# A decoder layer's output projection: operand sums and weight lo parts on VectorE, embedding lo parts by adding DMAs, weight sums in smaller steps

## The chip, the cores and the metric

One core of one Trainium2 chip. The metric is the device time of one execution in microseconds; a figure for a kernel is the median of several runs. The engines are named as in the profile: PE (TensorE matmul), PEld (its weight loads), DVE (VectorE), ACT (ScalarE), POOL (GpSimd) and SP (SyncE, which here only issues DMAs). "SPq", "ACTq" and "POOLq" are DMA issues of these engines. Every engine runs its own row of instructions in order.

## What is computed

One layer of a decoder trunk over 1024 positions of width 1024, all in float32: three kinds of attention heads side by side, whose 1024 outputs go through `w_out`; then a gated MLP with a causal convolution; then a gate on a per-layer embedding.

```
z = rmsnorm(h, norm_mix_g[l]) @ w_in[l]
...
o_a = hgrn2_mix(a_q, a_f, a_i, a_g, lbs[l], hgrn_gnorm_g[l])
o_b = dilated_window_mix(b_q, b_k, b_v)
...
h = h + jnp.concatenate([o_a, o_b.astype(o_a.dtype), o_c.astype(o_a.dtype)], axis=-1) @ w_out[l]
h = h + conv_glu_ffn(rmsnorm(h, norm_ffn_g[l]), ffn_up[l], ffn_conv_w[l], ffn_conv_b[l], ffn_down[l])
gate = jax.nn.sigmoid(rmsnorm(h, norm_ple_g[l]) @ ple_gate[l])
h = h + gate * (p[l] @ ple_proj[l])
```

## The kernel before

Activations lie transposed, 128 channels by 1024 positions to a tile (`T`), in halves of 512 (`HT`). Every float32 operand of a matmul is split in a hi part, which ACT casts (L124 for weights, L1296 for activations, L1482 for the embedding), and a lo part, the rest of it. A product is then three matmuls: hi x hi, lo x hi, hi x lo. For weights, `split2` makes the lo part in one of two ways. Given an engine, that engine subtracts (L130). Given a DRAM address, ACT negates the hi part (L127), and a POOL DMA adds the weight from DRAM once more onto it (L128).

The kernel's stages, with their times in the profile: the RWKV heads with the `w_in` projection (`project_rest`, to about 330 us), the other heads (to 572), the output projection (`phase_out`, to 661), part of the embedding product (`embed`, to 682), the MLP (up to about 1300), the gate.

**Output projection.** `w_out` is applied by seven products of half size instead of eight (Strassen's way), on sums of the operands and of the weight blocks. There are 28 jobs, in the order p1, p5, p3, p6, p7, p2, p4 with four blocks each, and every job is 12 matmuls of 128x512, 2.72 us on PE without waits. Job n's weight is loaded and split when job n - 4 is run (`weight`, L1342). The raw weights lie in halves of a ring of two 512 KB tiles (`wraw`); the four raw tiles of the embedding (`praw`) use the same ring, between the weights of jobs 18 to 27. Jobs of the products p1, p6, p7 and p4 run in banks that lie in pairs in one PSUM tile, so that the second job of a pair starts only behind the `gather` of the first, a DVE addition to the residual `h` (L1387). Gathers of p6 and p7 are followed by a square on ACT (L232) and its addition to `acc` on DVE (L233); PE sums `acc` over the channels (L200), DVE and POOL make the factor of the norm (L203, L207) and PE spreads it (L213). This is done once for the first half of the positions behind job 20, and once for the second half inside `embed`.

The work beside a job stands in a table: `at(n, steps)` puts step i behind job n + i. `pair` casts and subtracts to make hi and lo parts of an operand. `o_done`, called where a head group's output is ready, makes sums of operands for the first four blocks (`Eo[i]`, by a DVE subtraction and two ACT negations) and, for the last four, two POOL DMAs that add one block to the negated one (L1320, SBUF to SBUF). `turn4` subtracts on DVE for p4. `ffn_first` (L1534) loads the first four 512 KB tiles of `ffn_up` and splits them; it is put behind a job of the projection.

**Weight sums.** `out_sums` is a generator that builds four sums of `w_out` blocks for each of four block rows, in DRAM-loaded tiles: loads on SP (L457, L458), ACT negations in place, POOL DMAs that add (L455), and stores to the DRAM buffers `ws..` on SP (L463, L466, L475, L476). `project_rest` takes one step of it after k-steps 1, 3 and 6 of the eight of a `w_in` block. Beside it, on the same SP row, stand the loads of `w_in` (L115), the moves of the projections `z` (L505), and the two moves Tz (L743) and Tc (L748) by which a triangular matrix of the RWKV heads passes through DRAM. PE's L848 waits for Tc.

## Time and profile before

| | |
|---|---|
| median of 3 runs | 1424.47 us (1424.16 to 1427.31) |
| the profiled execution | 1429.45 us |
| its span in the trace | 1427.7 us |
| mean granted clock of TensorE | 0.985 |
| PE busy | 1376.9 us (96%) |
| DVE busy | 1062.1 us (74%) |
| ACT busy | 663.1 us (46%) |
| POOL busy | 382.5 us (27%) |
| bytes moved by DMA | 195.93 MB |

PE is busy for 96% of the span, so what is left to win are its waits and the time at which the throttle grants it less than full clock. A matmul group's row in the timeline gives start, length, what it writes and reads, how often it stands there (x2), and in square brackets how long PE was idle ahead of it and whose end released it. A row of the waits sums such idle time by the waiting line and the releaser. The row of a window gives busy time of each engine in a stretch, then the granted clock (1.00 is full) and the share of time in which the 16 DMA engines were busy.

### The profile page before, as it was taken

To read this page: it belongs to the slowest core of one execution; us is meant where nothing else is said; L and a number is where in the kernel's file an instruction comes from. 1 tells how busy PE (TensorE), PEld (TensorE's weight loads), DVE (VectorE), ACT (ScalarE), POOL (GpSimd) and SP (SyncE) were. 2 spreads that over 40 slices of the span, in tenths; PEclk is the share of its full clock that TensorE was granted. 3 is DMA by queue.
4 is the path that set the end of the run, shared out by engine and by line. 5 is a ranking of instruction groups with operands and counts; after the bars stand their busy time and mean duration, and the time that the engine had idled before them with its cause. 6 is when DMAs were issued, how large, how long until landed. Compare 5 with 4: busy or idle time off the path is not lost.

```text
span 1427.7 us, 22537 instructions
## 1 busy us (share of the span) xinstructions
PE 1376.9 (96%) x8598; PEld 1114.9 (78%) x8598; DVE 1062.1 (74%) x1652; ACT 663.1 (46%) x1143; POOL 382.5 (27%) x312
## 2 busy tenths in 40 slices
PE   8999999989999999988999999999999999999997
PEld 6878777867878777766788888888888888888886
DVE  7595456815657696667988889888988799777675
ACT  7523424233255584554644444344444444455662
POOL 4210112211221222321244445454543000002231
PEclk9999999999999999997999999999999999999998
DMA  6344533774732223894323232333233973352674
GB/s 227 89 118 112 134 111 92 176 168 115 237 116 97 90 65 84 212 295 124 137 74 107 101 109 97 111 111 110 89 111 119 353 243 104 109 164 62 174 194 146
DMA packets 98843, 195.93 MB, mean 137 GB/s; under 512 B 22064, under 2 KB 24368, under 8 KB 98736
## 3 DMA queue, kind: packets, MB, share of 16 engines
q1 hardware_dynamic: 73408, 155.44, 32.1%
q0 software_dynamic: 14256, 27.79, 11.0%
q10 hardware_dynamic: 11072, 11.28, 2.5%
q8 instruction: 67, 1.10, 0.3%
q14 instruction: 40, 0.33, 0.1%
HBM read 141.78 MB, written 50.59 MB: 135 GB/s over the span
## 4 chain that ended last, share of the span: by engine, by line
PE 51%; POOL 0%; DVE 0%; issue 0%; DMA 0%; POOLq 0%; ACT 0%; DVEq 0%
PE bg L1501 16%; PE bv L1501 12%; PE bv L1803 7%; PE bg L1803 7%; PE bv L152 1%; PE bv L154 1%; PE bv L156 1%; PE bg L152 1%; PE bg L156 1%; PE bg L154 1%; DMA raw<-in_ffn_up_dram 0%; PE dp L154 0%; PE dp L152 0%; PE dp L156 0%; POOL h L1892 0%
## 5 line engine op out<-in xcount | busy, mean ns | idle before, releaser
L130 POOL TENSOR_TENSOR wlo<-raw,whi 128x512 fp32r<-128x512 f32 x84 | 136.2, 1640 | 75.5 <-ACT whi L124 75.5
L124 ACT CAST whi<-wraw 128x512 fp32r<-128x512 f32 x120 | 73.3, 617 | 156.8 <-PE dp L154 99.8
L152 PE MATMUL dp<-xh,whi 128*128 128x512 f32 x416 | 139.6, 411 | 2.8 <-ACT xh L424 2.0
L154 PE MATMUL dp<-xl,whi 128*128 128x512 f32 x416 | 132.9, 394 | 0.9 <-DVE xl L425 0.9
L1501 PE MATMUL bg<-t,whi 128*128 128x512 f32 x352 | 133.2, 389 | 0.0
L156 PE MATMUL dp<-xh,wlo 128*128 128x512 f32 x416 | 132.4, 393 | 0.0
L130 POOL TENSOR_TENSOR wlo<-s,whi 128x512 fp32r<-128x512 f32 x44 | 65.4, 1486 | 170.0 <-ACT whi L124 170.0
L124 ACT CAST whi<-raw 128x512 fp32r<-128x512 f32 x88 | 52.6, 619 | 97.4 <-issue 51.5
L1803 PE MATMUL bg<-t,whi 128*128 128x512 f32 x308 | 95.1, 390 | 0.0
L1803 PE MATMUL bv<-t,whi 128*128 128x512 f32 x308 | 94.9, 389 | 0.0
L124 ACT CAST whi<-s 128x512 fp32r<-128x512 f32 x66 | 38.9, 619 | 118.8 <-PE bg L1501 113.5
L154 PEld LDWEIGHTS dp<-xl,whi 128*128 128x128 f32 x416 | 78.8, 189 | 18.8 <-DVE xl L425 1.8
L156 PEld LDWEIGHTS dp<-xh,wlo 128*128 128x128 f32 x416 | 78.4, 189 | 18.9 <-issue 1.5
L152 PEld LDWEIGHTS dp<-xh,whi 128*128 128x128 f32 x416 | 75.2, 190 | 22.9 <-issue 5.6
L1501 PEld LDWEIGHTS bg<-t,whi 128*128 128x128 f32 x352 | 66.0, 188 | 13.7
L207 POOL TENSOR_TENSOR rst<-rst,mhalf 128x4 f32<-128x4 f32 (+1 forms) x9 | 10.2, 1134 | 239.6 <-DVE rst L203 223.8
L128 POOL DMA_DIRECT2D wlo<-in_w_in_dram x28 | 25.3, 915 | 179.4 <-ACT wlo L127 156.4
L1799 ACT CAST t<-t 128x512 fp32r<-128x512 f32 x77 | 47.8, 622 | 45.7 <-PE bv L1803 32.6
L1501 PE MATMUL bg<-t,wlo 128*128 128x512 f32 x176 | 67.3, 389 | 0.0
L1803 PEld LDWEIGHTS bv<-t,whi 128*128 128x128 f32 x308 | 57.8, 188 | 12.0
L1803 PEld LDWEIGHTS bg<-t,whi 128*128 128x128 f32 x308 | 57.8, 188 | 11.9
L1800 DVE TENSOR_TENSOR t<-t,t 128x512 fp32r<-128x512 f32 x77 | 54.9, 713 | 8.0 <-ACT t L1799 7.8
(463 smaller groups left out, 3731.7 us busy)
## 6 DMA issues: line engine op xcount, KB each, us to landing
raw<-in_ffn_up_dram SPq DMA_DIRECT2D x44, 512.0 KB, 3.4
wraw<-in_w_in_dram SPq DMA_DIRECT2D x28, 512.0 KB, 3.8
z<-zst SPq DMA_DIRECT2D x18, 512.0 KB, 3.4
gb<-ct SPq DMA_DIRECT2D x33, 256.0 KB, 2.3
t<-gb SPq DMA_DIRECT2D x33, 256.0 KB, 2.8
t<-gt SPq DMA_DIRECT2D x33, 256.0 KB, 2.7
zl<-z SPq DMA_DIRECT2D x16, 512.0 KB, 4.4
wraw<-in_ple_gate_dram SPq DMA_DIRECT2D x16, 512.0 KB, 3.7
```

Source lines behind the costliest of these rows:

```text
L124: self.cast = nc.scalar.copy(hi, src).ins
L128: nc.gpsimd.dma_start(lo, eng, accum_op=ALU.add)
L130: eng.tensor_tensor(lo, src, hi.bitcast(F32), ALU.subtract)
L152: nc.tensor.matmul(ps[hf], wh, xh[hf], start=first, stop=False)
L154: nc.tensor.matmul(ps[hf], wh, xl[hf], start=False, stop=False)
L156: self.step = nc.tensor.matmul(ps[hf], wl, xh[hf], start=False, stop=last).ins
L207: nc.gpsimd.tensor_tensor(r2, r, self.mhalf[:, :n], ALU.pow)
L1501: self.step = nc.tensor.matmul(ps, w[part == 2][:, s], X[k][part == 1], start=start and k == part == 0, stop=k == 3 and part == 2, skip_gr ...
L1799: nc.scalar.copy(xh, x)
L1800: V.tensor_tensor(xl, x, xh.bitcast(F32), ALU.subtract)
L1803: nc.tensor.matmul(ps[m], wt[part == 2][:, m * P:(m + 1) * P], (xh, xl)[part == 1], start=k == part == 0, stop=k == NK - 1 and part == 2)
```

## The change

Five edits. The weight sums (`out_sums`) start after 9 pauses and not 15, are taken after every odd k-step (four to a block and not three), and one block row takes 14 steps and not 7, with pauses between loads, negations, adds and stores. In `o_done` one of the two ACT negations goes, the other becomes a copy, and the two POOL DMAs go; in their place `less` subtracts on DVE in `phase_out`, ahead of the pairs that use the sum. These pairs start behind jobs 6, 13 and 10 in place of 7, 10 and 11, and `turn4` behind job 16 in place of 12. All 28 weights of the projection get their lo part from DVE; so far the last twelve got it by L127 and L128. The embedding's lo parts are now negated on ACT and completed by an adding POOL DMA from DRAM (new L1489 and L1490), and no longer subtracted on DVE. `ffn_first` moves from behind job 15 to behind job 23.

```diff
--- before.py
+++ after.py
@@ -115,7 +115,7 @@
         nc.sync.dma_start(raw, src)
         return self.split_w(raw, src)
 
-    WB = 6
+    WB, LEAD = 6, 9
 
     def split2(self, src, eng):
 
@@ -442,37 +442,43 @@
 
         nc, wo = self.nc, self.a["w_out"]
         self.S = [{n: self.zpool.tile([P, HT], F32, tag=f"ws{n}{i}", name=f"ws{n}{i}") for n in "1234"} for i in range(4)]
-        for _ in range(15):
-            yield
+        def pause(n):
+            for _ in range(n):
+                yield
+
+        def turn(x):
+            nc.scalar.activation(x, x, AF.Copy, scale=-1.0)
+
+        def add(x, src):
+            nc.gpsimd.dma_start(x, src, accum_op=ALU.add)
+
+        yield from pause(self.LEAD)
         for i in range(4):
             a11, a12, a21, a22 = (wo[m][:, c] for m in (i, 4 + i) for c in (slice(0, HT), slice(HT, T)))
             t, u = (self.spool.tile([P, HT], F32, tag="sqt", name=self.nm("wsum"), bufs=2) for _ in (0, 1))
-
-            def turn(x):
-                nc.scalar.activation(x, x, AF.Copy, scale=-1.0)
-
-            def add(x, src):
-                nc.gpsimd.dma_start(x, src, accum_op=ALU.add)
-
             nc.sync.dma_start(t, a21)
             nc.sync.dma_start(u, a22)
-            yield
+            yield from pause(2)
             turn(t)
             add(u, a21)
             yield
+            add(t, a11)
+            yield from pause(2)
             nc.sync.dma_start(self.S[i]["1"], u)
-            add(t, a11)
             yield
             nc.sync.dma_start(self.S[i]["3"], t)
+            yield
             turn(u)
             yield
             turn(t)
             add(u, a11)
             yield
             add(t, a22)
+            yield
             add(u, a12)
+            yield from pause(2)
+            nc.sync.dma_start(self.S[i]["2"], t)
             yield
-            nc.sync.dma_start(self.S[i]["2"], t)
             nc.sync.dma_start(self.S[i]["4"], u)
             yield
 
@@ -489,7 +495,7 @@
                 self.mm3({0: ps[:, :HT], 1: ps[:, HT:]}, w(k), self.X[k], k == 0, k == ND - 1)
                 if k == 3 and i + 1 < len(js):
                     nxt = self.load_w(self.a["w_in"][js[i + 1]])
-                if k in (1, 3, 6):
+                if k % 2:
                     with self.behind(self.step):
                         next(self.sums, None)
                 yield
@@ -1309,15 +1315,12 @@
             nc.vector.tensor_tensor(t1, o[1], o[0], ALU.subtract)
             self.pair(self.A[i], o[0])
             self.pair(self.B[i], t1)
-            nc.scalar.activation(t1, t1, AF.Copy, scale=-1.0)
-            nc.scalar.activation(t3, o[1], AF.Copy, scale=-1.0)
+            nc.scalar.copy(t3, o[1])
             return
         i = self.LAST.index(k)
         for c in (0, 1):
             if (k, c) not in self.parts:
                 nc.scalar.copy(self.final(k, c, None), o[c])
-        for t in self.Eo[i][::-1]:
-            nc.gpsimd.dma_start(t, self.parts[k, 1], accum_op=ALU.add)
 
     def phase_out(self, hp, x0, emb):
 
@@ -1340,7 +1343,7 @@
                 hold.extend((t[:, left], t[:, right]))
             t, d = hold.pop(0), src[n](i)
             nc.sync.dma_start(t, d)
-            return self.split2(t, V if (n, i) in jobs[:16] else d)
+            return self.split2(t, V)
 
         g1 = [self.dps.tile([P, T], F32, tag="dp", name=self.nm("dp")) for _ in (0, 1)]
         banks = {"a": {i: g1[i // 2][:, (left, right)[i % 2]] for i in range(4)}, "b": {}, "c": {}}
@@ -1390,6 +1393,9 @@
                 if n in ("p6", "p7"):
                     sums(m, late)
 
+        def less(i, n):
+            V.tensor_tensor(Eo[i][n], Lo[i][1], Eo[i][n], ALU.subtract)
+
         def turn4(i):
             V.tensor_tensor(Lo[i][0], Lo[i][0], Eo[i][0], ALU.subtract)
 
@@ -1403,10 +1409,10 @@
         at(5, [lambda i=i: (empty("p1", i), load("p3", i)) for i in range(4)])
         at(16, [lambda i=i: load("p4", i) for i in range(4)])
         at(3, [lambda i=i: self.pair(D[i], Lo[i][1]) for i in range(4)])
-        at(7, [lambda i=i: self.pair(A[i], Eo[i][0]) for i in range(4)])
-        at(10, [lambda i=i: self.pair(C[i], Lo[i][0]) for i in range(4)])
-        at(11, [lambda i=i: self.pair(B[i], Eo[i][1]) for i in range(4)])
-        at(12, [lambda i=i: turn4(i) for i in range(4)])
+        at(6, [lambda i=i: (less(i, 0), self.pair(A[i], Eo[i][0])) for i in range(4)])
+        at(13, [lambda i=i: self.pair(C[i], Lo[i][0]) for i in range(4)])
+        at(10, [lambda i=i: (less(i, 1), self.pair(B[i], Eo[i][1])) for i in range(4)])
+        at(16, [lambda i=i: turn4(i) for i in range(4)])
         at(17, [lambda i=i: self.pair(A[i], Lo[i][0]) for i in range(4)])
         px, pw = [], []
         r = []
@@ -1446,7 +1452,7 @@
         for m in range(ND):
             sums(m, 1)
         ps, pb = small()
-        with self.behind(self.ends[15]):
+        with self.behind(self.ends[23]):
             self.ffn_first()
         r = []
         hooks = {(1, 0): lambda: r.append(self.rstd(ps, (acc,))), (1, 1): lambda: self.rstd_spread(r[0], pb)}
@@ -1480,7 +1486,8 @@
         hi, lo = (pool.tile([P, T], F32R, name=self.nm(n)) for n in ("peh", "pel"))
         for c in (slice(0, HT), slice(HT, T)):
             self.nc.scalar.copy(hi[:, c], raw[:, c])
-            self.nc.vector.tensor_tensor(lo[:, c], raw[:, c], hi[:, c].bitcast(F32), ALU.subtract)
+            self.nc.scalar.activation(lo[:, c], hi[:, c].bitcast(F32), AF.Copy, scale=-1.0)
+            self.nc.gpsimd.dma_start(lo[:, c], self.a[src][k][:, c], accum_op=ALU.add)
         dst.append((hi, lo))
 
 
```

Three places of the engines' rows show what moves; the lines of the changed program lie a few further on (L1296 becomes L1302, L1387 L1390, L1389 L1392, L1482 L1488, L1520 L1527, L1527 L1534).

The first is ACT's row around job 20, the last of p2. `peh` and `pel` are hi and lo parts of the embedding, here of `ple_proj`; `sqt` with `h7` is the last square of the first half, `whi` and `wlo` belong to the weight of job 23, `hd` are copies of `h` to DRAM. Before:

```order
L124 CAST whi_1118_6485<-wraw_1111_6449 128x512
L1389 DMA hd7_0_5953<-h7_5938 128x512
L127 ACTIVATE wlo_1119_6487<-whi_1118_6485 128x512
L232 ACTIVATE sqt_1120_6504<-h7_5938 128x512
L1296 CAST xh_897_5386<-xh_921_5410 128x512
L1389 DMA hd0_1_5940<-h0_5931 128x512
L1482 CAST peh_1116_6478<-praw_1115_6476 128x512 x2
```

After:

```order
L124 CAST whi_1118_6477<-wraw_1111_6439 128x512
L1302 CAST xh_897_5386<-xh_921_5410 128x512
L1488 CAST peh_1116_6468<-praw_1115_6466 128x512 x2
L1489 ACTIVATE pel_1117_6469<-peh_1116_6468 128x512 x2
L1392 DMA hd7_0_5941<-h7_5926 128x512
L232 ACTIVATE sqt_1120_6495<-h7_5926 128x512
```

The last square of the first half stood ahead of the cast of the embedding, and stands behind it and its negation now; the negation of the weight is gone.

The second is DVE's row from the gather of job 23 (L1387, from the tile `zo`) to that of job 24 (from `dp`); the rows between are parts of the norm of the first half (L1527) and the lo parts `t` of its results (L1520). Before:

```order
L1387 TENSOR_TENSOR h3_5934<-h3_5934,zo_1144_6619 128x512
L1527 SCALAR_TENSOR_TENSOR h2_5933<-h2_5933,par_78,ps_ss_1132_6551 128x512
L1520 TENSOR_TENSOR t1_1090_6389<-h0_5931,t0_1089_6388 128x512
L1527 SCALAR_TENSOR_TENSOR h3_5934<-h3_5934,par_78,ps_ss_1132_6551 128x512
L1520 TENSOR_TENSOR t3_1092_6391<-h1_5932,t2_1091_6390 128x512
L1387 TENSOR_TENSOR h4_5935<-h4_5935,dp_1026_5972 128x512
```

After:

```order
L1390 TENSOR_TENSOR h3_5922<-h3_5922,zo_1144_6611 128x512
L1527 TENSOR_TENSOR t1_1090_6377<-h0_5919,t0_1089_6376 128x512
L1527 TENSOR_TENSOR t3_1092_6379<-h1_5920,t2_1091_6378 128x512
L130 TENSOR_TENSOR wlo_1143_6609<-wraw_1138_6579,whi_1142_6607 128x512
L1534 SCALAR_TENSOR_TENSOR h2_5921<-h2_5921,par_78,ps_ss_1132_6546 128x512
L1534 SCALAR_TENSOR_TENSOR h3_5922<-h3_5922,par_78,ps_ss_1132_6546 128x512
L1390 TENSOR_TENSOR h4_5923<-h4_5923,dp_1026_5960 128x512
```

The lo part of job 27's weight (L130) is new between the two gathers.

The third is DVE's row from the gather of the last job, 27, to the factor of the norm of the second half (L203). L130 are lo parts of the MLP's first weights, from `ffn_first`. Before:

```order
L1387 TENSOR_TENSOR h7_5938<-h7_5938,dp_1027_5973 128x512
L233 TENSOR_TENSOR acc_5955<-acc_5955,sqt_1147_6715 128x512
L130 TENSOR_TENSOR wlo_1161_6746<-raw_1156_6736,whi_1160_6744 128x512
L233 TENSOR_TENSOR acc_5955<-acc_5955,sqt_1148_6718 128x512
L130 TENSOR_TENSOR wlo_1187_6953<-raw_1154_6732,whi_1186_6951 128x512
L233 TENSOR_TENSOR acc_5955<-acc_5955,sqt_1149_6721 128x512
L130 TENSOR_TENSOR wlo_1189_6957<-raw_1156_6736,whi_1188_6955 128x512
L233 TENSOR_TENSOR acc_5955<-acc_5955,sqt_1150_6724 128x512
L1623 TENSOR_TENSOR s6_1193_7156<-s6_1193_7156,raw_1154_6732 128x512
L233 TENSOR_TENSOR acc_5955<-acc_5955,sqt_1151_6727 128x512
L203 TENSOR_SCALAR rst_1165_6775<-ps_ss_1152_6730 128x4
```

After:

```order
L1390 TENSOR_TENSOR h7_5926<-h7_5926,dp_1027_5961 128x512
L233 TENSOR_TENSOR acc_5943<-acc_5943,sqt_1149_6713 128x512
L130 TENSOR_TENSOR wlo_1161_6738<-raw_1156_6728,whi_1160_6736 128x512
L233 TENSOR_TENSOR acc_5943<-acc_5943,sqt_1150_6716 128x512
L130 TENSOR_TENSOR wlo_1187_6945<-raw_1154_6724,whi_1186_6943 128x512
L233 TENSOR_TENSOR acc_5943<-acc_5943,sqt_1151_6719 128x512
L130 TENSOR_TENSOR wlo_1189_6949<-raw_1156_6728,whi_1188_6947 128x512
L203 TENSOR_SCALAR rst_1165_6767<-ps_ss_1152_6722 128x4
```

Up to the last addition to `acc`, two additions of squares, a lo part and a sum of the MLP's weights (L1623) have left this stretch. In PE's row, L200 of the second half stands ten matmuls earlier and L213 six matmuls earlier in the embedding's product. On SP, in the RWKV heads' first group, two stores of weight sums that stood elsewhere lie between Tz and Tc.

## The prediction

> **What bounds the kernel now.** I read TensorE's idle time and its granted clock by stretches first. The columns are stretch, length, busy time of PE, PEld, DVE, ACT and POOL (with instructions), then granted clock, DMA share and GB/s.
>
> ```profile
> 600.00:700.00 100.00, 86.47 (x345) 67.90 (x346) 74.12 (x119) 57.74 (x98) 15.03 (x15) 0.90 0.66 200
> 800.00:900.00 100.00, 100.00 (x443) 82.81 (x442) 88.27 (x89) 40.61 (x57) 51.82 (x33) 1.00 0.29 100
> ...
> 292.00:308.00 16.00, 11.52 (x186) 9.22 (x185) 0.92 (x2) 5.76 (x11) 1.76 (x2) 0.79 0.96 199
> 598.00:608.00 10.00, 7.22 (x25) 5.49 (x24) 7.12 (x12) 7.15 (x15) 2.40 (x3) 0.83 0.89 231
> 640.00:656.00 16.00, 10.47 (x28) 7.87 (x29) 9.43 (x15) 8.34 (x16) 1.73 (x2) 0.68 0.57 128
> 667.00:680.00 13.00, 11.16 (x41) 8.65 (x42) 9.53 (x17) 3.33 (x5) 1.04 (x1) 0.74 0.43 163
> 712.00:720.00 8.00, 6.24 (x21) 4.89 (x21) 6.05 (x6) 2.12 (x3) 2.33 (x2) 0.79 0.09 35
> ```
>
> From 800 on PE is 100% busy at clock 1.00, so microseconds won before it stay won to the end. They can be won only where PE waits or runs slow, and 600 to 700 loses most: 13.5 idle and (1 - 0.90) x 100 = 10 of clock. The change's edits touch the five short stretches below that. In them the clock costs (1 - clock) x length: 3.4, 1.7, 5.1, 3.4 and 1.7 us.
>
> The waits of TensorE come next (what waits, for what, total us, times, longest):
>
> ```profile
> PE dp L1501 <- DVE h L1387: 6.9, 6, 2.8
> PE dp L1501 <- DMA wlo<-in_w_out_dram: 4.7, 1, 4.7
> ```
>
> **The weights' lo parts: removed.** The timeline (start, length, engine, instruction, idle before and its releaser) shows the 4.7 us wait and what makes it.
>
> ```profile
> 636.07 1.19 ACT L124 CAST whi<-wraw 128x512 fp32r<-128x512 f32 x2 [1.27 <-DMA wraw<-in_w_out_dram]
> ...
> 637.17 1.15 ACT L127 ACTIVATE wlo<-whi 128x512 fp32r<-128x512 f32 x2
> ...
> 638.10 1.81 POOL L128 DMA_DIRECT2D wlo<-in_w_out_dram  x2 [5.69 <-ACT wlo L127]
> ...
> 639.32 0.39 PE L1501 MATMUL dp<-xh,whi 128*128 128x512 f32 x1
> ...
> 644.65 0.79 PE L1501 MATMUL dp<-xh,wlo 128*128 128x512 f32 x1 [4.72 <-DMA wlo<-in_w_out_dram]
> ```
>
> The hi part stands at 637.26. The lo part takes a negation on ACT, an issue on POOL and an adding DMA, and PE has it at 644.65. After the change DVE subtracts right behind the cast:
>
> ```profile
> L130 DVE TENSOR_TENSOR wlo<-wraw,whi 128x512 fp32r<-128x512 f32 x8 | 5.5, 686 | 0.9 <-ACT whi L124 0.9
> ```
>
> At 686 ns both lo parts would be there about 638.7, before job 24's start at 639.32. So 4.72 of waiting and the 5.1 of clock behind it go: **-9.8**.
>
> **The same edit: what comes late next.** (a) The first L200 column sum waits for the last square of the first half.
>
> ```profile
> 629.41 1.14 ACT L1482 CAST peh<-praw 128x512 fp32r<-128x512 f32 x2 [0.97 <-DMA praw<-in_ple_proj_dram]
> ...
> 629.66 1.05 PE L200 MATMUL ps_ss<-few,acc 128*128 128x1 f32 x8 [1.38 <-DVE acc L233]
> ```
>
> Before, that square stands on ACT ahead of this cast. After, it stands behind cast and negation, 1.14 + 1.15 = 2.3 us, which wait for the load of praw. If this load landed as now, the wait would grow by some 3.2; the two-tile ring frees earlier, because ACT and not DVE makes the lo parts, so I take 2.1 to 4.1 for the wait, middle 3.1: **+1.7**.
>
> (b) Gather 24 (DVE) must empty a bank that job 25 needs. The wait for it is now
>
> ```profile
> 650.16 0.77 PE L1501 MATMUL dp<-xh,whi 128*128 128x512 f32 x1 [0.87 <-DVE h L1387]
> ...
> 695.60 2.49 DVE L1520 TENSOR_TENSOR tp7l<-h,tp7h 128x512 fp32r<-128x512 f32 x4
> ```
>
> and DVE had stood idle ahead of it because of the 4.72. After, five operations lie between gathers 23 and 24, one of them the lo part of job 27. By the second row one takes 2.49 / 4 = 0.62, so 3.1 us, more than a job's 2.72; and the lo part waits for its cast and load. I take 1.9 to 3.8 in place of 0.87 for job 25 (**+2.0**), and **+0.7** for job 27. (c) Waits of this size have cost the clock elsewhere: behind the row at 601.32 below it fell to 0.83. I take about half of the 5.1 again: **+2.4**. The place together: -9.8 + 1.7 + 2.0 + 0.7 + 2.4 = **-3.0**; all of it kept is -9.8, and all the new waits at their high ends with the clock gone as now are about +2.
>
> The Trainium skill, "TensorE: Matmul & The Clock Gate", Part 1, says that the clock halves after one idle window of about 3.4 us and comes back after as long a busy time. Here it fell behind 2.78 and even behind 0.31 + 0.85 + 0.80, so the trace goes lower than that rule; by the rule, (c) would be nothing and the place -5.4.
>
> **Sums of the operands, and the first stall.** The eight SBUF-to-SBUF adding DMAs of L1320 and four ACT negations go, eight subtractions come to DVE (8 x 0.62 = 5.0), eight embedding subtractions leave it (5.0), twelve lo parts come (7.4). Net 7.4 us of DVE over some 24 jobs of 2.72, of which DVE has waits to spare (74 of 100 busy above): nothing on average. The one place where DVE is already late:
>
> ```profile
> 586.90 0.32 SPq L1342 DMA_DIRECT2D wraw<-ws  x1
> ...
> 596.23 0.62 ACT L124 CAST whi<-wraw 128x512 fp32r<-128x512 f32 x1 [2.86 <-DMA wraw<-ws]
> ...
> 600.58 0.68 DVE L1387 TENSOR_TENSOR h<-h,dp 128x512 f32<-128x512 f32 x1
> ...
> 601.32 0.50 PE L1501 MATMUL dp<-xh,whi 128*128 128x512 f32 x1 [2.78 <-DVE h L1387]
> ```
>
> The longest wait for a gather is this one. A 256 KB load took 9.3 us there, with the queues full (below). After, the lo parts of jobs 16 and 17 stand in DVE's row ahead of gathers 11 and 12, and inherit those late loads: up to 1.0 more wait, 2.5 with the clock. Against that, the adds of L1320 leave, the last of them just ahead of the stage's loads. The view of DMA from 580 to 640 has the busy share in tenths of 40 slices of 1.5 us, and then packets, MB and share by queue, of which q0 is the adding one:
>
> ```profile
> DMA  9999999999993997999999999999999869999799
> ...
> q1 hardware_dynamic: 4236, 9.80, 49.7%
> q0 software_dynamic: 2309, 4.20, 39.1%
> ```
>
> To 598 the twelve slices are full. 39.1 / 4.20 against 49.7 / 9.80 per MB makes an added byte 1.8 times as dear as a loaded one. Twelve lo adds (3.1 MB) and eight of L1320 (2.1 MB) go, eight for the embedding (2.1 MB) come. I take **0** for this stall, between -3.3 (the loads earlier by nearly all of it, with part of the clock) and +2.5. The Trainium skill, "DMA: Bandwidth & Descriptors", "Issuing engines are not separate DMA queues", says that transfers of all engines share the same 16 DMA engines and interleave. That speaks against turning the embedding's lo parts into adding DMAs; by it the loads of jobs 24 to 27 land later and the sum goes towards the slower rival.
>
> **The tail of the stage.**
>
> ```profile
> 661.48 0.69 DVE L1387 TENSOR_TENSOR h<-h,dp 128x512 f32<-128x512 f32 x1 [0.18 <-PE dp L1501]
> ...
> 668.50 0.68 DVE L233 TENSOR_TENSOR acc<-acc,sqt 128x512 f32<-128x512 f32 x1
> ...
> 669.24 1.05 PE L200 MATMUL ps_ss<-few,acc 128*128 128x1 f32 x8 [0.85 <-DVE acc L233]
> ...
> 671.66 1.11 PE L213 MATMUL ps_ss<-cst,rst 128*128 128x128 f32 x4 [0.80 <-POOL rst L207]
> ...
> 672.81 5.36 DVE L1527 SCALAR_TENSOR_TENSOR h<-h,par,ps_ss 128x512 f32<-128x512 f32 x8 [2.32 <-PE ps_ss L213]
> ...
> 713.86 0.50 PE L1501 MATMUL bv<-tp4h,whi 128*128 128x512 f32 x1 [1.76 <-DVE bv L1674]
> ```
>
> Behind the last gather DVE has nine operations up to the last sum of squares; after the change five. L200 stands ten matmuls (2.27 us) earlier in PE's row, and six matmuls lie between L200 and L213 in place of two. So the 0.85 and 0.80 go, and the 3.4 of clock with them: -5.1 at 675. But from 672.81 on DVE sets the start of bv, as it hardly rests:
>
> ```profile
> 690.00:700.00 10.00, 10.00 (x46) 8.29 (x45) 10.00 (x18) 8.33 (x15) 0.00 (x0) 1.00 0.65 215
> ```
>
>  It begins only as much earlier as L213 does, about 2.6, and has one sum (0.6) more in its way. So what lasts is **-2.5**, with 713.86 waiting longer. Ends: -5 if DVE's gaps take it up, -1 if the last square is late on ACT.
>
> **Weight sums.** Four steps to a block of eight in place of three, and starts and adds further apart.
>
> ```profile
> 282.30 0.32 SPq L466 DMA_DIRECT2D ws<-wsum  x1
> ...
> 285.17 0.46 SPq L743 DMA_DIRECT2D Tz<-Tb  x1
> ...
> 286.16 1.79 POOL L455 DMA_DIRECT2D wsum<-in_w_out_dram  x2
> ...
> 290.61 5.25 SPq L748 DMA_DIRECT2D Tc<-Tz  x4
> ...
> 298.11 0.24 PE L848 MATMUL py<-Tc,sc 32*32 32x32 f32 x2 [3.98 <-DMA Tc<-Tz]
> ```
>
> SP stood at 282.30 for the finished sum, behind it the 512 KB loads of the weight and z, and then Tz; Tz and two adds shared the queues, and Tc came 3.98 late. With 0.5 behind it and 3.4 of clock the place costs 7.9. After, the two stores wait for nothing, and the loads go out some 3 to 4 us earlier; the adds still fall near Tz. I take **-3.5**, between -8 and +1. At the earlier head group's Tc, which has no wait now, two stores now stand between Tz and Tc on SP: 0 to +2, taken as 0.
>
> Three small moves (a matmul group behind the wait at 546, gather 14, gnv's earlier place) I put at **0** together, within 1 either way. Moving the raw ffn loads behind job 23 costs nothing if they land before the tail's lo parts. In the view of DMA from 580 to 640,
>
> ```profile
> raw<-in_ffn_up_dram SPq DMA_DIRECT2D x4, 512.0 KB, 7.5
> ```
>
> so issued behind job 23 (639) they land about 647, and the tail's first lo part follows the gathers of jobs 24 to 26. If they come later than that, the tail loses its 2.5.
>
> **Sum:** -3.0 + 0 - 2.5 - 3.5 = -9.0 against the profiled execution's 1429.45 (span 1427.7 and 1.75 around it): 1420.45. The median of the runs, 1424.47, lies 4.98 below that execution, so the forecast of the median is 1415.5.
>
> **Rivals.** (1) *Full gain*: no new wait at L200 or job 25, the whole 9.8, 5 at the tail and 8 at Tc: about -20, 1404. For it: each wait named is short by only 1 to 3 us. Against: DVE's row at gather 24 is longer than a job. Chance 0.2. (2) *No change that can be told* (a measurement of this kernel tells about 0.2%, 2.85 us): the new waits eat the place of job 24, the clock halves as now, Tc comes as late since Tz still meets the adds, and the tail's DVE chain gives 1 to 2: about 1423. Chance 0.14. (3) *Slower*: lo parts on an in-order DVE make every late load of the two-tile ring block the gathers behind it, and so PE. It decides from landings above about 7.5 us for the loads of jobs 24 to 27. At the 9.3 of the row at 586.90, jobs 24 and 26 wait some 4 each at half clock (2 x (4 + 2.5) = 13, less 9.8 removed, and 2.5 lost at the tail by late squares): +5.7, or 1430. For it: 512 KB loads and adds of the embedding fall in that time; against: the DMA share falls to 0.57 by 640. Chance 0.14. (4) My forecast, one or two of the three places partly gained: 0.52.
>
> **How the numbers follow.** Forecast 1415.5, own range 1407 to 1421.5. With 8 in 10 the range leaves out half of the full gain's cases and most of the slower ones' far end: 1402 to 1427. Faster: 0.2 + 0.52 = 0.72; same 0.14; slower 0.14.
>
> **What would show it.** Right: no wait for wlo from DMA in the waits of PE; L200 after job 20 waits 2 to 4, job 25 about 2 to 4 for the gather; L200 after job 27 not at all, and bv near 713 more than 1.76; the Tc wait of 3.98 halved. Wrong: a wait of over 3 us for Tc; DVE idle for raw weights between 590 and 600 or 636 and 645 with PE behind it; a granted clock in 640 to 656 above 0.9 (full gain) or under 0.7 (slower).

## The result

| | median | runs | ratio to before, 95% interval |
|---|---|---|---|
| before | 1424.64 us | 6 (1422.35 to 1429.77) | |
| changed | 1418.14 us | 6 (1411.68 to 1419.59) | 0.9943 [0.9918, 0.9967] |

The change makes the kernel 6.5 us faster by the medians; the ratio in the table, which is an estimate from all runs and not the quotient of the medians, makes it 8.1 (0.57% of 1424.64). Forecast were 9.0 (1415.5), with a range of 1402 to 1427. The two profiled executions, at 1429.45 and 1418.19, differ by more, 11.3: a second profile of the kernel before took 1432.91, so both of its profiles are among its slower executions.

The stretches of the changed kernel that answer to those of before (columns as there):

```profile
288.00:304.00 16.00, 12.83 (x211) 10.06 (x210) 1.85 (x5) 6.15 (x12) 0.00 (x0) 0.89 0.63 151
592.00:602.00 10.00, 6.50 (x18) 4.79 (x17) 5.38 (x10) 4.01 (x8) 0.00 (x0) 0.68 0.49 170
636.00:652.00 16.00, 9.95 (x34) 7.71 (x33) 13.05 (x22) 9.91 (x19) 1.76 (x2) 0.79 0.85 273
655.00:672.00 17.00, 16.77 (x81) 13.66 (x80) 15.91 (x27) 7.27 (x10) 3.95 (x3) 1.00 0.32 127
700.00:720.00 20.00, 19.37 (x85) 15.29 (x83) 15.03 (x17) 9.58 (x13) 9.32 (x7) 1.00 0.15 52
```

and its waits of PE:

```profile
PE dp L1508 <- DVE h L1390: 12.8, 6, 6.0
...
PE py L854 <- DMA Tc<-Tz: 3.2, 2, 2.4
...
PE ps_ss L200 <- DVE acc L233: 2.1, 1, 2.1
```

The last two stretches, the tail, are clean now: PE is busy for nearly all of them and the clock is full. The stretch of job 24 is not: the 4.7 us for a lo part from a DMA is gone from the list, but waits for gathers have grown from 6.9 to 12.8 us. One of them is 6.0. PE's idle time in 636 to 652 is 6.05, against 5.53 in 640 to 656 before; the clock there is 0.79, against 0.68.

Starting points of three stages, in us from the start of the span, split the gain of the profiles:

| | job 4 starts | embedding starts | from there to the end |
|---|---|---|---|
| before | 573.90 | 661.28 | 766.4 |
| before, second profile | 575.14 | 664.64 | 766.5 |
| changed | 568.12 | 656.91 | 759.3 |

So 5.8 us were won ahead of the projection's job 4, where the weight sums are made; 1.4 were lost in jobs 4 to 27 (87.4 us before, 88.8 after; 89.5 in the second profile of before); and 7.1 were won behind them. This is the split of 11.5 us between two profiles; the section on the prediction says how much of it the medians bear out.

### The profile page after: what moved, and what is told of

It is laid out like the page before. It is cut to its first block, busy times and chain, and to the rows that moved or that the text cites. A ratio compares the mean times of both kernels' runs of the same rounds, so it can differ in the third digit from the quotient of the medians.

```text
span 1416.2 us, 22504 instructions
## 1 busy us (share of the span) xinstructions
PE 1371.1 (97%) x8598; PEld 1110.9 (78%) x8598; DVE 1064.9 (75%) x1664; ACT 657.7 (46%) x1135; POOL 368.7 (26%) x300
## 4 chain that ended last, share of the span: by engine, by line
PE 77%; DVE 9%; issue 8%; POOL 2%; ACT 2%; DMA 1%; SPq 0%; POOLq 0%; DVEq 0%; ACTq 0%
PE bg L1508 16%; PE bv L1508 12%; PE bv L1810 7%; PE bg L1810 7%; PE dp L152 6%; PE dp L154 5%; PE dp L156 5%; PE bv L152 1%; PE bv L154 1%; PE bv L156 1%; PE bg L152 1%; PE bg L154 1%; PE bg L156 1%; DVE ig L648 1%; PE zp L152 1%
## 5 line engine op out<-in xcount | busy, mean ns | idle before, releaser
L130 POOL TENSOR_TENSOR wlo<-raw,whi 128x512 fp32r<-128x512 f32 x84 | 134.2, 1617 | 76.6 <-ACT whi L124 76.5
L130 POOL TENSOR_TENSOR wlo<-s,whi 128x512 fp32r<-128x512 f32 x44 | 64.1, 1456 | 152.2 <-ACT whi L124 152.2
L130 DVE TENSOR_TENSOR wlo<-wraw,whi 128x512 fp32r<-128x512 f32 x74 | 53.3, 724 | 30.1 <-ACT whi L124 21.6
```

The lines of the kernel that those rows point to most:

```text
L130: eng.tensor_tensor(lo, src, hi.bitcast(F32), ALU.subtract)
```

## The experiments

The kernels are named by what they are. In the table stand the longest waits of PE at job 13 and in jobs 24 to 27, and the time from the embedding's start to the span's end, all from the profiles. The ratio is that to the kernel before on the same chip; medians of different sessions can differ by a few us where ratios don't.

| kernel | median us | ratio, 95% interval | job 13 | 24 to 27 | tail and rest |
|---|---|---|---|---|---|
| before | 1424.64 | | 2.78 | 4.72 | 766.4 |
| changed | 1418.14 | 0.9943 [0.9918, 0.9967] | 3.50 | 6.05 | 759.3 |
| sums_only | 1419.0 | 0.9960 [0.9945, 0.9974] | 2.51 | 4.84 | 763.6 |
| old_sums | 1421.91 | 0.9984 [0.9967, 1.0001] | 3.67 | 6.79 | 759.6 |
| emb_dve | 1415.17 | 0.9927 [0.9913, 0.9941] | 3.28 | 1.67 | 760.4 |
| ffn15 | 1419.13 | 0.9951 [0.9936, 0.9966] | 3.78 | 5.71 | 760.4 |
| ops_old | 1414.50 | 0.9919 [0.9900, 0.9938] | 4.59 | 3.86 | 758.2 |
| p4_pool | 1417.56 | 0.9934 [0.9912, 0.9955] | 4.75 | 5.98 | 759.4 |
| p7_pool | 1418.53 | 0.9943 [0.9924, 0.9963] | 5.43 | 2.83 | 760.4 |
| emb_pooladd | 1417.75 | 0.9936 [0.9921, 0.9950] | 3.50 | 6.04 | 759.3 |
| p7_add | 1416.59 | 0.9922 [0.9904, 0.9939] | 4.64 | 2.68 | 760.4 |
| ring3 | 1406.72 | 0.9855 [0.9836, 0.9874] | 1.19 | 1.12 | 759.3 |
| after_ring3 | 1412.12 | 0.9893 [0.9868, 0.9918] | 1.47 | 1.61 | 759.8 |

### The weight sums, alone and taken out

sums_only is the kernel before with this edit alone:

```diff
-            if k in (1, 3, 6):
+            if k % 2:
```

with the new `out_sums` and LEAD = 9.

> The kernel before with the new weight sums alone (start after 9 pauses, four steps to a block, 14 steps to a block row); nothing else of the change. Theory W: what the changed kernel gained ahead of job 12 (in the two profiles job 12 starts at 595.66 before and 589.89 after, 5.8 us) comes from the weight sums, mostly at the Tc wait of 3.98 and its clock. Then this is 3 to 6 us faster than before (about 1419 to 1421.5), PE's wait for Tc is under 2.5 in its profile and job 12 starts 4 to 6 earlier. Rival: the 5.8 come from the operand sums that left POOL and ACT, or are the scatter of one profiled execution; then this is within 1.5 us of before and its wait for Tc is 3 or more.

old_sums takes the same edit, all of it, out of the changed kernel.

> The changed kernel with the weight sums of before. Theory W: the wait for Tc is 4 or so again with its clock, and the time is 3 to 6 us above the changed kernel (1421 to 1424). Rival (gain elsewhere): within 1.5 us of the changed kernel.

Measured by the ratios: alone the edit gains 0.40% of the time before, 5.7 us, and old_sums loses as much against the changed kernel (0.9984 against 0.9943, 5.8 us; the two intervals meet at 0.9967, and the medians differ by 3.8). Theory W holds from both sides. The same run says something of the rest of the change: old_sums is the kernel before with the other four edits, and at 0.9984 [0.9967, 1.0001] these gain 2.3 us together, which can't be told from nothing. The timeline of sums_only shows the Tc wait shortened, that of old_sums shows it whole. Of sums_only:

```profile
291.79 0.24 PE L854 MATMUL py<-Tc,sc 32*32 32x32 f32 x2 [1.92 <-DMA Tc<-Tz]
...
293.12 0.34 PE L854 MATMUL py<-Tc,sc 32*32 32x32 f32 x10 [1.10 <-DMA Tc<-Tz]
```

and of old_sums:

```profile
296.08 0.31 PE L848 MATMUL py<-Tc,sc 32*32 32x32 f32 x2 [4.01 <-DMA Tc<-Tz]
```

With its clock that place gives about 3. On SP's row the load of a `w_in` weight now goes out 5.5 us ahead of Tz (275.62 and 281.13), and before it went out 0.9 ahead (284.25 and 285.17). Whether the earlier start, the finer steps or the wider pauses do this, no run separates. The rest is at two waits that I had not costed. Of the kernel before, the timeline around 148:

```profile
144.89 0.63 ACT L452 ACTIVATE wsum<-wsum 128x512 f32<-128x512 f32 x1 [0.72 <-DMA wsum<-in_w_out_dram]
...
148.41 0.62 ACT L124 CAST whi<-wraw 128x512 fp32r<-128x512 f32 x1 [2.90 <-DMA wraw<-in_w_in_dram]
...
149.92 0.29 PE L848 MATMUL sk<-ar,khat 64*64 64x128 f32 x1 [1.37 <-DVE MG L944]
```

and the same cast in the changed kernel:

```profile
145.13 0.62 ACT L124 CAST whi<-wraw 128x512 fp32r<-128x512 f32 x1 [1.19 <-DMA wraw<-in_w_in_dram]
```

Before, the loads for a sum were issued on SP at 139.64 and 140.12, ahead of a `w_in` weight at 141.15. That weight's cast stood ready on ACT 7.3 us after its issue, and everything behind it on ACT, and so PE, waited 1.37. Now the sum's loads go out at 146 and 148, the cast comes 4.2 us after its load's issue (140.92), and PE has no wait there. The other is the yt wait, before and after:

```profile
203.87 0.63 PE L828 MATMUL yt<-cst,y 128*128 128x128 f32 x4 [1.88 <-DVE y L822]
...
199.62 0.63 PE L834 MATMUL yt<-cst,y 128*128 128x128 f32 x4 [0.67 <-DVE y L828]
```

Both follow the edit: sums_only has no wait at the first place and 0.67 at the second, old_sums has 1.20 and 1.88.

### The embedding's lo parts back on DVE

```diff
-            self.nc.scalar.activation(lo[:, c], hi[:, c].bitcast(F32), AF.Copy, scale=-1.0)
-            self.nc.gpsimd.dma_start(lo[:, c], self.a[src][k][:, c], accum_op=ALU.add)
+            self.nc.vector.tensor_tensor(lo[:, c], raw[:, c], hi[:, c].bitcast(F32), ALU.subtract)
```

> The changed kernel with the embedding's lo parts on DVE as before; eight adding DMAs (2.1 MB) leave the queues, eight DVE operations come back. Theory D: job 25 waits 6.05 us because DVE's own row is full and in order (lo part 26 ahead of gather 23, five operations to gather 24). Then eight more DVE operations leave that wait at 5 or more and the time at 1417 to 1422. Theory L: the wait comes from loads that land late beside the embedding's adds (raw weights of jobs 24 to 27). Then the landings of these loads fall below 4.5, the wait for gather 24 falls to 3 or less, and the time is 2 to 5 below the changed kernel (1413 to 1416).

The measured 1415.17 lies in theory L's interval, though the intervals of the two ratios overlap (0.9927 against 0.9943). The profiles show more: jobs 4 to 27 take 84.7 us here and 88.8 in the changed kernel. First the changed kernel's timeline. Raw weights of jobs 24 and 25 are issued at 624.18, those of 26 and 27 at 635.11:

```profile
624.18 1.35 SPq L1345 DMA_DIRECT2D wraw<-in_w_out_dram  x2
...
633.74 0.62 ACT L124 CAST whi<-wraw 128x512 fp32r<-128x512 f32 x1 [1.79 <-DMA wraw<-in_w_out_dram]
...
634.39 0.69 DVE L130 TENSOR_TENSOR wlo<-wraw,whi 128x512 fp32r<-128x512 f32 x1 [1.72 <-ACT whi L124]
...
635.11 0.83 SPq L1345 DMA_DIRECT2D wraw<-in_w_out_dram  x2
...
639.29 0.62 ACT L124 CAST whi<-wraw 128x512 fp32r<-128x512 f32 x1 [1.69 <-DMA wraw<-in_w_out_dram]
...
639.94 0.69 DVE L130 TENSOR_TENSOR wlo<-wraw,whi 128x512 fp32r<-128x512 f32 x1 [1.89 <-ACT whi L124]
640.55 0.68 DVE L1390 TENSOR_TENSOR h<-h,zo 128x512 f32<-128x512 f32 x1
...
644.27 0.68 DVE L1390 TENSOR_TENSOR h<-h,dp 128x512 f32<-128x512 f32 x1
...
645.09 0.77 PE L1508 MATMUL dp<-xh,whi 128*128 128x512 f32 x1 [6.05 <-DVE h L1390]
```

Read it upwards. PE waits for gather 24 (644.27); gather 23 (640.55) and the rest of DVE's row waited for lo part 26 (639.94), this for a cast and a load (635.11), and the load was not issued before lo part 25 had freed the raw tile (634.39), which was cast 9.6 us after the issue of its pair. In emb_dve the same pairs are issued at 625.89 and 632.84 and cast at 630.27 and 635.87:

```profile
625.89 0.81 SPq L1345 DMA_DIRECT2D wraw<-in_w_out_dram  x2
...
630.27 1.12 ACT L124 CAST whi<-wraw 128x512 fp32r<-128x512 f32 x2
...
642.48 0.47 PE L1507 MATMUL dp<-xh,whi 128*128 128x512 f32 x1 [1.67 <-ACT t L1525]
```

Here the casts follow 4.4 us behind the issue and not 9.6, and PE's wait is 1.67: with 2.1 MB of adds from POOL alongside, the loads that SP had issued took longer. The Trainium skill's "DMA: Bandwidth & Descriptors", "Issuing engines are not separate DMA queues", says that DMAs interleave on the same 16 DMA engines whichever engine issued them, and these rows agree.

### The MLP's first loads behind job 15 again

```diff
-        with self.behind(self.ends[23]):
+        with self.behind(self.ends[15]):
```

> The changed kernel with the first MLP weights behind job 15 again, as before. Theory F: the tail's gain (in the profiles 9.4 - 4.4 = 5.0 us between the start of the embedding and its fourth block) comes from moving these loads and their lo parts; then L200 and L213 of the second half wait again (0.85 and 0.80), the clock falls, and the time is 4 to 6 above the changed kernel (1422 to 1424). Theory G: it comes from the lo parts of the last twelve weights having left ACT and POOL, so that the last squares and sums follow each other faster; then L200 waits for nothing here either, and the time is within 1.5 of the changed kernel.

1419.13, within 1.0 of the changed kernel, and the time from the embedding's start to the end is 760.4 against 759.3. Theory F falls: the tail's gain does not come from moving these loads. Theory G has its time, but its cause, the lo parts, isn't shown by this run alone, and its "waits for nothing" was too strong: L200 of the second half does wait there (1.37), and so does bv (1.39), but no clock is lost behind either.

### The operand sums made as before

ops_old is emb_dve with the ACT negations, the eight SBUF-to-SBUF adds and the old places of pairs and `turn4`, without `less`.

> The previous experiment with the embedding's lo parts on DVE (emb_dve), and now the sums of the operands made as before, too: two ACT negations, eight adding DMAs on POOL, no subtraction (less) on DVE, pairs and turn4 behind the jobs of before. What is left of the change is the weight sums, all 28 weight lo parts on DVE and the later MLP loads. Theory O: the first stall, before job 13 (2.78 before, 3.28 to 3.78 in every kernel with less), is long because less and the lo part of a later weight stand ahead of gather 12 on DVE; without less it is 2.8 or shorter, and the time is 1 to 2.5 below emb_dve's 1415.2. Rival: the adds on POOL delay the raw weights at the stage's start, so the stall is 3.3 or more and the time is equal or 1 to 3 above emb_dve.

Theory O falls: without `less` the wait at job 13 is 4.59, longer and not shorter, while the time is 0.7 lower, inside the interval. As a whole the operand sums' edit is worth nothing that these runs can tell.

### Where does job 25 wait?

p4_pool gives the lo parts of jobs 24 to 27 to POOL:

```diff
-            return self.split2(t, V)
+            return self.split2(t, V if (n, i) in jobs[:24] else G)
```

> The changed kernel, with the lo parts of the last four weights (jobs 24 to 27) subtracted on POOL and no longer on DVE, the embedding's adds kept. Theory D (DVE's own row, where lo part 26 stands ahead of gather 23): no lo part blocks a gather there, the wait of 6.05 at job 25 falls to 2 or less, and the time falls by 3 to 6 against the changed kernel (1412 to 1415). Theory L (late loads beside the adds): the loads stay late, so PE waits as long for hi or lo parts of weights 25 to 27, and the time stays within 2 of the changed kernel or above it.

The wait stays (5.98), and the time is within 0.6 of the changed kernel. Theory D falls as the only cause: with DVE's lo parts gone, the same late raw weight (cast at 641.60, 3.7 us after its issue at 637.93) holds ACT's row, where a cast that DVE needs stands behind it. PE starts when gather 24 (646.36) ends.

```profile
641.60 0.62 ACT L124 CAST whi<-wraw 128x512 fp32r<-128x512 f32 x1 [1.81 <-DMA wraw<-in_w_out_dram]
642.12 1.13 ACT L1526 CAST t<-h 128x512 fp32r<-128x512 f32 x2
...
642.76 3.02 DVE L1527 TENSOR_TENSOR t<-h,t 128x512 fp32r<-128x512 f32 x2 [1.15 <-ACT t L1526]
...
646.36 0.67 DVE L1390 TENSOR_TENSOR h<-h,dp 128x512 f32<-128x512 f32 x1
...
647.18 0.76 PE L1508 MATMUL dp<-xh,whi 128*128 128x512 f32 x1 [5.98 <-ACT t L1526]
```

Some of the 5.98 comes from the experiment itself: the two lo parts at 642.76 take 3.02 us beside POOL's subtractions, against 1.28 in the changed kernel (641.15). Without that 1.7 the wait would still be over 4, where theory D asked for 2 or less.

emb_pooladd keeps ACT's negation and adds on POOL from the raw tile, so that no adding DMA is left for the embedding:

```diff
-            self.nc.gpsimd.dma_start(lo[:, c], self.a[src][k][:, c], accum_op=ALU.add)
+            self.nc.gpsimd.tensor_tensor(lo[:, c], lo[:, c].bitcast(F32), raw[:, c], ALU.add)
```

> The changed kernel, with the embedding's lo parts still begun by ACT's negation, but completed by an addition on POOL from the raw tile in place of the adding DMA. ACT's extra work stays, the 2.1 MB of adds leave the queues, and the raw tile is held longer. Theory L (the adds delay the raw weights of jobs 24 to 27): the loads of these weights, 9.5 us from issue to cast in the changed kernel, take under 6, the wait at job 25 (6.05) falls to 3 or less, and the time to 1414 to 1416.5. Rival N (ACT's eight negations, 4.9 us, delay squares and casts): the wait stays above 4.5 and the time within 1417 to 1421.

By the time (1417.75) and the wait (6.04) this is the rival's result, by the rows it is neither's:

```profile
630.94 0.80 SPq L1345 DMA_DIRECT2D wraw<-in_w_out_dram  x2
...
633.80 0.62 ACT L124 CAST whi<-wraw 128x512 fp32r<-128x512 f32 x1 [3.84 <-PE zo L1508]
```

The loads take at most 2.9 us here (the cast waited for PE and not for its load), as theory L said of a queue without adds, but they are issued at 630.94, 6.8 later than in the changed kernel: POOL's additions hold the raw tiles of the embedding for longer. Late landing and late release end in the same wait; that both do so by turning the ring of two raw tiles more slowly is argued from the rows. A part is again POOL's: DVE's lo part at 640.89 takes 1.75 us beside its additions.

### The first stall and the ring

p7_pool and p7_add are emb_dve with another lo part for jobs 16 to 19: by POOL, and as before the change by ACT and an adding DMA.

```diff
-            return self.split2(t, V)
+            return self.split2(t, G if n == 'p7' else V)
```

> The kernel emb_dve with the lo parts of the weights of jobs 16 to 19 on POOL in place of DVE. Theory O2: the first stall comes from such a lo part standing ahead of gather 12 on DVE with its load late; without it the stall falls from 3.28 to 2.5 or less, with less clock lost, and the time is 1 to 3 below emb_dve. Rival: POOL's subtraction (some 1.3 to 1.6 us beside DVE) slows DVE's own operations by as much, or PE waits for the lo parts: within 1 of emb_dve, or above.

```diff
-            return self.split2(t, V)
+            return self.split2(t, d if n == 'p7' else V)
```

> The kernel emb_dve with the lo parts of jobs 16 to 19 made as before the change: negated on ACT and completed by an adding DMA from DRAM, so that the two-tile ring of raw weights is freed by the cast and not by the subtraction. Theory R (the subtraction holds the raw tile, so that the next loads are issued later, and the first stall follows from it: 3.28 with DVE, 5.43 with the slower and later POOL): the stall is 2.8 or less and the time 1 to 2.5 below emb_dve's 1415.2. Rival: four adds come back into the stage's start, where the queues are full; the stall is 3 or more and the time equal or above.

Both make the wait at job 13 longer (5.43 and 4.64), and neither makes the kernel faster than emb_dve by more than the intervals (0.9943 and 0.9922 against 0.9927). So theory O2 falls: neither way of taking the lo part out of DVE's order shortens this wait. Theory R's form for p7_add falls too: freeing the tile by the cast did not help where the lo part needs an adding DMA; that full queues are the reason is the rival's argument and was not tested apart. The rows of p7_pool show what stays without a lo part on DVE:

```profile
590.77 0.62 ACT L124 CAST whi<-wraw 128x512 fp32r<-128x512 f32 x1 [2.86 <-DMA wraw<-ws]
591.30 0.62 ACT L1302 CAST xh<-xl 128x512 fp32r<-128x512 f32 x1
...
591.95 1.36 DVE L1303 TENSOR_TENSOR xl<-xl,xh 128x512 fp32r<-128x512 f32 x1 [2.03 <-ACT xh L1302]
```

A weight's cast waits 2.86 on ACT for a late load, an operand's cast stands behind it, and DVE, whose gathers PE needs, waits 2.03 for that. (Its own 1.36 is beside POOL's subtraction; the same operation takes 0.68 in emb_dve.) So a late load reaches the gathers through ACT's row, whichever engine makes the lo part.

ring3 turns to the ring itself: three raw tiles. The room comes from the split weights, five pairs in place of six.

```diff
-    WB, LEAD = 6, 9
+    WB, LEAD = 5, 9
...
-                t = self.wpool.tile([P, T], F32, tag="wraw", name=self.nm("wraw"), bufs=2)
+                t = self.wpool.tile([P, T], F32, tag="wraw", name=self.nm("wraw"), bufs=3)
```

> The kernel emb_dve with three raw tiles in the ring in place of two; for their room five split weights are kept in place of six (the weight of the job and the four ahead of it). Theory R: loads are issued earlier, the first stall (3.28) falls below 2 and the wait for the Tc rows is unchanged; time 1 to 4 below emb_dve. Rival (the first stall is set by the queues, full at the stage's start): the stall stays at 3 or more; and where the sixth split weight was needed, waits for casts appear elsewhere (the MLP) and the time rises.

1406.72, 8.5 us below emb_dve; in ratios to before 0.9855 against 0.9927, which is more than was expected. Between 580 and 592 no cast of a weight waits for its load. The timeline has the waits at jobs 13 and 25, of 1.19 and 0.87,

```profile
591.98 0.50 PE L1507 MATMUL dp<-xh,whi 128*128 128x512 f32 x1 [1.19 <-DVE h L1390]
...
633.67 0.47 PE L1507 MATMUL dp<-xh,whi 128*128 128x512 f32 x1 [0.87 <-DVE h L1390]
```

and the clock stays at 1.00 from 588 to 644. Jobs 4 to 27 take 77.2 us from job 4's start to the embedding's, 84.7 in emb_dve. The tail is as in the changed kernel. Five split weights were not run without the third tile.

after_ring3 is the changed kernel with the same two edits, the embedding's adding DMAs kept.

> The changed kernel itself, with three raw tiles in the ring and five split weights, so with the embedding's adding DMAs, which ring3 has not (1406.7). Theory R3: the adds cost the changed kernel its 3 us only by loads that land late in a ring of two; with a third tile the waits at job 13 (3.50) and job 25 (6.05) fall below 1.5 each, and the time is within 1.5 of ring3 (1405.5 to 1408.5). Rival: the adds cost PE time of themselves (ACT's negations ahead of squares and casts, or queues so full that three tiles don't cover a load); then a wait of 3 or more stays at job 25 or at L200 and the time is 2.5 or more above ring3 (over 1409).

Both long waits are gone (1.47 and 1.01), as theory R3 said, and the time falls by 0.5% of before against the changed kernel (0.9893 against 0.9943). But it is 0.38% above ring3, so that R3 falls for the time. The profile has part of it in the clock: L200 waits 1.98 and the clock halves behind it; ring3's L200 waits 1.67 and it doesn't. The stretch around that wait in after_ring3 (columns as above):

```profile
620.00:632.00 12.00, 10.02 (x37) 7.96 (x36) 4.69 (x8) 6.07 (x12) 4.64 (x6) 0.72 1.07 292
```

and in ring3:

```profile
617.00:629.00 12.00, 9.66 (x48) 7.56 (x47) 10.49 (x19) 7.53 (x14) 1.41 (x1) 1.00 0.86 298
```

That is (1 - 0.72) x 12 = 3.4 us, with the DMA engines full (1.07) in the kernel with the adds. Whether this clock loss comes in every execution, and whether the rest of the difference lies at Tc (4.04 there and 2.84 in ring3), these two profiles don't settle.

### The kernel before once more

> The kernel before once more, for a second profile. If the 1429.45 of its first profile, 5 above the median, is scatter of single executions, this one lies within 1422 to 1428, with the same waits (Tc about 4, first stall 2.8, lo part of job 24 4.7, 0.85 and 0.80 in the tail) and other ones ahead of 200 us; if the profile itself costs time, it lies near 1429 again.

1432.91 with the waits of the first profile, two of them longer: 5.13 at Tc and 3.63 at job 13. The prediction of 1422 to 1428 missed. The timed runs of this kernel reach from 1421.93 to 1433.26 in these sessions, so 1432.91 is within its scatter. Whether a profile costs it time stays open; the changed kernel's profiled 1418.19 equals its median.

## Why the prediction came out right, step by step

The sum was right in sign and within its range, and its three large terms were each of another size.

Put together, the four terms as the two profiles show them give -5.8 - 0.5 + 2.2 - 7.1 = -11.2, near the profiles' difference of 11.3 and more than the 6.5 to 8.1 of the runs. With the tail at the -4.3 that sums_only leaves it (below) they give -8.4. The four edits other than the weight sums, forecast at -5.5, then come to -2.6, near the 2.3 of old_sums, whose interval reaches 0. So -9.0 came close because misses of both signs cancelled: the weight sums and the tail gave more than forecast, the place of job 24 gave almost nothing, and the first stall was longer in this profile. That they cancelled is luck. The range, 1402 to 1427, was also wide enough to hold the median of the kernel before.

**Weight sums: -3.5 forecast, -5.7 and -5.8 measured.** The mechanism at Tc was right (the load that left Tz's neighbourhood, above), and that term was about right in size: idle 4.48 and clock 3.4 before, 3.17 and 1.8 after, a difference of 2.9. The longest wait did not quite halve, 3.98 to 2.36. What was missing are the waits at 149.92 and 203.87. I had put everything outside Tc at 0 without looking at what the loads of the sums do to the weights that are issued behind them.

**The place of job 24: -3.0 forecast, nothing gained.** The removal came as worked out: no wait for a lo part from a DMA is left. Step (a), L200, waits 2.12, at the low end of the 2.1 to 4.1. Step (b) failed: 1.9 to 3.8 forecast, 6.05 measured. I counted the operations between gathers 23 and 24, and these take what I said (640.55 to 644.27). But the longest part lay ahead of gather 23, where lo part 26 waited for its load and the load for the tile. That is the chain of the slower rival, and its condition was met: a landing above 7.5, with 9.6 for weight 25. The prediction's own sign of being wrong showed too, DVE idle for raw weights between 636 and 645 with PE behind it (1.89 at 639.94). It cost the place nearly all it had won, but not more, since job 27 waits 0.87 as before. In the prediction's terms: -9.8 + 0.7 for L200 + 5.2 for job 25 + 0 for job 27 + 3.4 of clock = -0.5.

**The first stall: 0 forecast, between -3.3 and +2.5.** It is 3.50 after 2.78, and its clock costs 3.2 where it cost 1.7, together 2.2 more: near the upper end. The cause named, lo parts ahead of the gathers on DVE, is not shown: p7_pool takes the lo parts of jobs 16 to 19 off DVE and the wait is longer, with the late loads now coming through ACT's casts. It shrinks to 1.19 with a third raw tile. The second profile of before has 3.63 at this place, so a difference of 0.7 between single profiles is not a finding.

**The tail: -2.5 forecast, -7.1 between the profiles, -4.3 against sums_only.** The embedding's start to the end is 766.4 and 766.5 before, 759.3 after. L200 and L213 came forward, L213 by 3.6 where 2.6 was worked out (10.4 us from the embedding's start before, 6.8 after). What failed is the step "what lasts is -2.5", by which DVE's row would hold bv back: its wait of 1.76 at 713.86 was to grow, and it is gone from the changed kernel's timeline. The step was read from a stretch in which DVE is full (690 to 700). But behind the norms it had stood idle. In the timeline of before, ACT's row,

```profile
681.98 1.01 ACT L1471 COPY pst<-dp 128x1024 f32<-128x1024 f32 x1 [0.68 <-PE dp L156]
682.89 0.62 ACT L1519 CAST tp6h<-nu 128x512 fp32r<-128x512 f32 x1
```

and DVE's:

```profile
683.55 0.69 DVE L1520 TENSOR_TENSOR tp6l<-nu,tp6h 128x512 fp32r<-128x512 f32 x1 [2.37 <-ACT tp6h L1519]
```

DVE waited 2.37 for a cast that stood on ACT behind a copy of PE's embedding block, and PE had been at half clock from 671 to 677. After, PE is not slowed, and the same wait in its timeline is

```profile
674.13 0.69 DVE L1527 TENSOR_TENSOR tp6l<-nu,tp6h 128x512 fp32r<-128x512 f32 x1 [0.19 <-ACT tp6h L1526]
```

So the engine that I took as the bound was itself waiting for the one that I had freed. Of what made the tail faster, sums_only (763.6, with 0.85 and 0.80 still there) has 2.8 without any edit in the tail: the clock fell for less time there, and behind the bv wait of 1.79 it did not fall at all. That part is no finding for the change. The other 4.3 fall to the lo parts of the weights, by exclusion only: old_sums, without the new weight sums, has 759.6; ffn15, without the moved loads, 760.4; ops_old, with the weight sums, the lo parts and the later loads alone, 758.2. A kernel with the lo parts as its only edit was not run.

**The embedding's adds: no term, one sentence.** They cost about 0.16% of before (0.9943 against 0.9927), whose intervals overlap, and 0.38% with three tiles (0.9893 against 0.9855), whose intervals meet only at their ends. That the operand sums come to nothing was right.

## What to carry to other kernels

A lo part that is subtracted from the raw tile holds it until the subtraction; with a ring of two, a late load, a slow subtraction and a busy queue all end in the same wait, and one more tile, with one split weight fewer, was worth more here (8.5 us between the medians) than any choice of the engine. When an edit removes a wait, look past it for the load whose issue depends on the same tile, and count from its issue to its landing in the fullest stretch. Before calling an engine the bound, look whether its own idle time ends at the engine that the edit frees.

## What the runs showed of the hardware beyond that

In these profiles the clock doesn't follow the length of a wait: behind 2.12 us at the changed kernel's L200 (and 2.59 in emb_dve) it stayed at 1.00 from 620 to 632, behind 1.98 us at the same place of after_ring3 it was 0.72 over the same stretch. The Trainium skill, "TensorE: Matmul & The Clock Gate", Part 1, says that the clock falls after an idle window of about 3.4 us and that this window runs freely. That a wait's place in the window decides would fit these rows, but none shows the window, and the rule's 3.4 us is longer than any of these waits.

A subtraction on DVE beside an addition on POOL was slower: in emb_pooladd,

```profile
619.26 1.73 POOL L1490 TENSOR_TENSOR pel<-pel,praw 128x512 fp32r<-128x512 f32 x1
619.77 1.78 DVE L1400 TENSOR_TENSOR xh<-xh,xh 128x512 f32<-128x512 f32 x1
```

against 0.69 for the same DVE operation in the changed kernel (620.67).
